# A two-layer decoder trunk with routed experts: weights laid out in load order, one transfer per tile

## The chip, the cores and the metric

The kernel runs on one core of a Trainium2 chip. The metric is device time in microseconds of one execution. The time before is the median of three runs, 851.8 us (851.02 to 852.24).

## What is computed

The reference is a trunk of two layers over 256 tokens of width 1024, in float32. Each layer has a mixer (a combined input projection, a causal convolution branch, a pooling branch, gates, an output projection) and a channel mixer with 32 experts, of which each token uses two. Both are scaled and shifted by vectors that come from `c` through `w_ada`. Cut to what matters:

```python
c_act = jax.nn.silu(c)
for l in range(2):
    sh1, sc1, g1, sh2, sc2, g2 = jnp.split(c_act @ w_ada[l] + b_ada[l], 6, axis=-1)
    proj = modulate(rms_norm(x, mixer_norm_g[l]), sh1, sc1) @ w_in[l]
    u_conv, u_pool, gates = proj[..., :1024], proj[..., 1024:1536], jax.nn.sigmoid(proj[..., 1536:])
    gate_a, gate_b = jnp.split(gates, 2, axis=-1)
    y_a = conformer_conv_branch(u_conv, ...)       # ends in @ w_conv_out
    y_b = pool_branch(u_pool, pool_w[l], pool_scale[l])
    x = x + g1 * ((gate_a * y_a + gate_b * y_b) @ w_out[l])
    t = modulate(rms_norm(x, ffn_norm_g[l]), sh2, sc2)
    # combine: weight of each token for each expert, zero but for two experts of one group
    for e in range(32):
        act = jax.nn.silu(t @ w_expert_gate[l, e]) * (t @ w_expert_up[l, e])
        x = x + g2 * ((act * combine[:, e, None]) @ w_expert_down[l, e])
return rms_norm(x, final_norm_g)
```

The weights are float32 and each is read once; most of the bytes are the experts' (64 experts of 3 MB), then `w_ada`.

## The kernel before

**The stream of weights.** Before any work is written down, `plan` (L84) fills a list, `stream`, with every weight tile of both layers in the order of use. A tile is 128 partitions x 2048 floats, 1 MB. Per layer these are six vectors of `w_ada` at 4 tiles each (`plan_ada`, key `ada`), 14 tiles of `w_in` (`plan_in`, `in`), one of `pool_w` (`pw`), 2 of `w_conv_out` and 4 of `w_out` (`plan_out`, `co`, `wo`), and for each of 16 pairs of experts four gate/up tiles (`gu`, for half h of the contraction and each expert of the pair) and two down tiles (`ed`), by `plan_pair`. Some `ada` tiles of layer 1 stand before layer 0's experts.

**Buffers.** `room` (L92) gives a tile one of 14 ring buffers (`wt` in the profile), or, for expert tiles, one of five work buffers that are idle then (`wx`; the table `SPARE`). `issue` (L102) walks the list in order and writes a transfer on SP's queue for each tile for which there is room; `done` (L122) marks a tile as used and calls `issue` again. So SP's instructions stand in the order of the list, and each waits until the last reader of its buffer has finished. `trickle` puts small loads (rows of biases, the router) between them.

**Form of the transfers.** The host lays out `w_in`, `pool_w` and the small tables (`laid_out`, L1254); the other weights are read from their own arrays. A tile of `w_ada`, `w_conv_out`, `w_out` or `w_expert_down` is one transfer whose rows are two runs of 4 KB per partition. A `gu` tile takes two transfers, one from `w_expert_gate` and one from `w_expert_up`, each of 512 KB with a run of 4 KB per partition; the tile then holds gate and up side by side. The last pair's two down tiles each hold one half of the columns of both experts, in pieces of 2 KB and two transfers.

**Completion semaphores.** Transfers from SP and from ACT signal one of eight semaphores (`DMAHW0` to `DMAHW7`), given in turn in the order in which they are written down, whichever of the two queues issues them. A transfer that gets a semaphore again waits until the one eight places before it has landed.

**The use.** In the mixer each tile is split into two float32r parts on ACT and VectorE or GpSimd (L412, L414) before TensorE uses it in three products. In the experts (`blocks`, L1108, an order written by hand for TensorE, VectorE and ACT) a pair b of experts runs two halves of gate and up products (L1118), SiLU and the product (L1126, L1127), the scatter of the pair before (L1073, L1074), a transpose (L1133), then the down products (L1093). The `gu` tiles of a half are free after that half, the `ed` tiles after the down products.

**`final_norm_g`.** In layer 1, behind pair 5, `final_gain` (L1199) loads `final_norm_g` into the buffer `fz` by a transfer on ACT's queue (L1204). It stands among ACT's instructions of that pair.

**Overflow.** `overflow` holds a branch for tokens beyond an expert's 64 places, with its own weight loads on GpSimd's queue.

Of the kernel before, what the change touches and what calls it, by code (L numbers as in the profile page):

```python
# [29 lines left out]
NE = NG * EPG  # L30
DE = 256
# [17 lines left out]

@with_exitstack  # L50
def trunk(ctx, tc, x, c, w_ada, b_ada, w_in, ada_cols, mix_rows, router, pool_w, w_conv_out, w_out,
          w_expert_gate, w_expert_up, w_expert_down, final_norm_g, out):
# [23 lines left out]
    stream = []  # L76
# [24 lines left out]

    def issue():  # L102
        while state["issued"] < len(stream):
            key, src, (a, b), q = stream[state["issued"]]
            t = room(key, q)
            if t is None:
                return
            v = t[:, :a * b].rearrange("p (a b) -> p a b", b=b)
            if isinstance(src, tuple):
                v = v.rearrange("p (i k) h -> p i k h", i=2)  # L110
                for i, sr in enumerate(src):
                    nc.sync.dma_start(out=v[:, i], in_=sr)
# [11 lines left out]
        issue()  # L124

    def plan_ada(l, m, part=range(4)):
        v = w_ada[l].rearrange("(p k) n -> p k n", k=KC)
        for i in part:
            plan(("ada", l, m, i), v[:, 2 * i:2 * i + 2, m * D:(m + 1) * D], (2, D))

    def plan_in(l, g):
        shape = (KC, 256) if g < 2 else (4, 512)
        for i in range(2):
            yield ("in", l, g, i), w_in[l, 2 * g + i].rearrange("p (a b) -> p a b", b=shape[1]), shape

    def plan_out(l):
        for nm, w, n in (("co", w_conv_out, 2), ("wo", w_out, 4)):
            v = w[l].rearrange("(j p) n -> p j n", p=P)
            for i in range(n):
                plan((nm, l, i), v[:, 2 * i:2 * i + 2, :], (2, D))  # L140

    def plan_pair(l, e):
        ents = []
        for h in range(2):
            for j in range(2):
                ents.append((("gu", l, e + j, h),
                             tuple(w[l, e + j].rearrange("(p k) h -> p k h", k=KC)[:, 4 * h:4 * h + 4, :]
                                   for w in (w_expert_gate, w_expert_up)), (KC, DE)))
        wd = w_expert_down[l, e:e + 2].rearrange("e (j p) n -> p e j n", p=P)
        for j in range(2):  # L150
            if e + 2 < NE:
                ents.append((("ed", l, e + j), wd[:, j], (2, D)))
            else:
                ents.append((("ed", l, e + j), tuple(wd[:, z, :, 512 * j:512 * j + 512] for z in range(2)), (4, 512)))
# [9 lines left out]
    for l in range(DEPTH):  # L164
        for a in pre[l]:
            plan_ada(*a)
        ents = [e for g in groups for e in plan_in(l, g)]
        ents[1], ents[2] = ents[2], ents[1]
        in_seq[l] = [e[0] for e in ents]
        plan_ada(l, 2, range(lead[l]))  # L170
        for n, e in enumerate(ents):
            plan(*e)
            if n == 0:
                plan_ada(l, 2, range(lead[l], 4))
            if n == 12:
                plan(("pw", l), pool_w[l].rearrange("p (g o) -> p g o", o=256), (4, 256))
# [808 lines left out]
    def overflow(l, r, moe):  # L985
# [3 lines left out]
        with (tc.If(flag > 0, label="ov0") if l == 0 else tc.If(flag > 0)):  # L989
# [3 lines left out]
            wsp = r["XTW"][1].rearrange("p a c -> p (a c)")  # L993
# [4 lines left out]
            for tt in range(TT):  # L998
# [9 lines left out]
                                                op0=OP.mult, op1=OP.add)  # L1008
                for e in range(NE):
                    p = pa([P, 2, DE])  # L1010
                    for i, wsrc in enumerate((w_expert_gate, w_expert_up)):
                        wv = wsrc[l, e].rearrange("(p k) h -> p k h", k=KC)
                        for h in range(2):
                            w = wsp.rearrange("p (k h) -> p k h", h=DE)
                            nc.gpsimd.dma_start(out=w, in_=wv[:, 4 * h:4 * h + 4, :])
# [216 lines left out]
    for l in range(DEPTH):  # L1232
# [14 lines left out]


_INS = ['x', 'c', 'w_ada', 'b_ada', 'w_in', 'ada_cols', 'mix_rows', 'router', 'pool_w', 'w_conv_out', 'w_out',
        'w_expert_gate', 'w_expert_up', 'w_expert_down', 'final_norm_g']  # L1250
_OUTS = [((1, SEQ, D), 'float32')]


def laid_out(inputs):  # L1254
# [15 lines left out]
    o = 0  # L1270
# [34 lines left out]
```

## Time and profile before

| | |
|---|---|
| median of 3 runs | 851.8 us |
| profiled execution, its own time | 852.07 us |
| span of the profiled execution | 850.2 us |
| granted TensorE clock, mean | 0.972 |
| PE / VectorE / ACT / GpSimd busy | 778.5 / 505.6 / 277.0 / 198.2 us |
| moved by DMA | 298.39 MB, mean 351 GB/s |

In the order of time: the first vectors of `w_ada` and the norm (to about 35 us), layer 0's mixer (to about 185), routing, layer 0's experts (about 207 to 432), layer 1's mixer (about 444 to 585), routing, layer 1's experts (about 614 to 839), the final norm. [...]

### The profile page before, as it was taken

To read this page: it belongs to the slowest core of one execution; us is meant where nothing else is said; L and a number is where in the kernel's file an instruction comes from. 1 tells how busy PE (TensorE), PEld (TensorE's weight loads), DVE (VectorE), ACT (ScalarE), POOL (GpSimd) and SP (SyncE) were. 2 spreads that over 40 slices of the span, in tenths; PEclk is the share of its full clock that TensorE was granted. 3 is DMA by queue.
4 is the path that set the end of the run, shared out by engine and by line. 5 is a ranking of instruction groups with operands and counts; after the bars stand their busy time and mean duration, and the time that the engine had idled before them with its cause. 6 is when DMAs were issued, how large, how long until landed. Compare 5 with 4: busy or idle time off the path is not lost. (4 is left out here: it accounts for less than half of the span.)

```text
span 850.2 us, 11978 instructions
## 1 busy us (share of the span) xinstructions
PE 778.5 (92%) x4382; PEld 454.4 (53%) x4382; DVE 505.6 (59%) x1023; ACT 277.0 (33%) x494; POOL 198.2 (23%) x133
## 2 busy tenths in 40 slices
PE   4599999997899999999879999999779999999985
PEld 2389986755333433343349998686523333333432
DVE  2369984976344644545376997497734554544545
ACT  2254544434122222222145454543322222222212
POOL 1258972510000000000034898161000000000001
PEclk9699999999999999999989999999889999999998
DMA  9999758969999999999999954797579998999993
GB/s 358 413 421 411 270 174 333 358 238 403 393 409 408 409 410 402 409 409 409 403 417 420 381 182 149 293 385 256 193 264 366 409 405 316 408 410 408 409 408 119
DMA packets 78080, 298.39 MB, mean 351 GB/s; under 512 B 7349, under 2 KB 7861, under 8 KB 74426
## 3 DMA queue, kind: packets, MB, share of 16 engines
q1 hardware_dynamic: 77448, 296.44, 89.6%
q10 hardware_dynamic: 434, 1.06, 0.3%
q8 instruction: 37, 0.61, 0.3%
q14 instruction: 33, 0.27, 0.1%
q0 software_dynamic: 128, 0.02, 0.0%
HBM read 296.44 MB, written 1.05 MB: 350 GB/s over the span
## 5 line engine op out<-in xcount | busy, mean ns | idle before, releaser
L1118 PE MATMUL pb<-wt,XTW 128*64 128x512 f32 x872 | 219.6, 593 | 12.9 <-DMA wt<-in_w_expert_up_dram 8.2
L414 POOL TENSOR_TENSOR wlo<-wt,whi 128x1024 fp32r<-128x1024 f32 x60 | 147.3, 2466 | 88.5 <-ACT whi L412 64.8
L1118 PEld LDWEIGHTS pb<-wt,XTW 128*64 128x64 f32 x872 | 73.6, 137 | 131.3 <-issue 124.5
L1127 DVE SCALAR_TENSOR_TENSOR sl<-sl,rtile,pb 128x256 f32<-128x256 f32 x32 | 15.4, 480 | 164.4 <-ACT sl L1126 164.4
L473 DVE SCALAR_TENSOR_TENSOR pd<-vpad,cols,pd 128x256 f32<-128x256 f32 x232 | 106.9, 488 | 5.7
L412 ACT CAST whi<-wt 128x1024 fp32r<-128x1024 f32 x80 | 82.8, 1049 | 73.8 <-PE pb L352 40.8
L1093 PE MATMUL pd<-wt,aT 128*64 128x512 f32 x360 | 102.7, 618 | 1.8 <-DVE aT L1135 0.5
L1100 ACT CAST yhl<-y 128x512 fp32r<-128x512 f32 x64 | 39.6, 619 | 137.9 <-DVE y L1099 137.9
L351 PE MATMUL pa<-hhl,whi 128*128 128x256 f32 x224 | 66.7, 298 | 5.2 <-ACT hhl L386 5.2
L1126 ACT ACTIVATE sl<-pb 128x256 f32<-128x256 f32 x32 | 12.3, 385 | 172.7 <-PE pb L1118 172.7
L352 PE MATMUL pa<-hhl,whi 128*128 128x256 f32 x224 | 65.6, 293 | 0.3
L353 PE MATMUL pa<-hhl,wlo 128*128 128x256 f32 x224 | 64.5, 288 | 0.6 <-POOL wlo L414 0.6
L351 PE MATMUL pb<-hhl,whi 128*128 128x256 f32 x224 | 63.6, 284 | 0.0
L297 PE MATMUL pd<-wt,cb 128*32 128x512 f32 x384 | 51.4, 623 | 13.1 <-DMA wt<-in_w_ada_dram 13.0
L352 PE MATMUL pb<-hhl,whi 128*128 128x256 f32 x224 | 62.7, 280 | 0.0
L353 PE MATMUL pb<-hhl,wlo 128*128 128x256 f32 x224 | 62.6, 279 | 0.0
L1093 PEld LDWEIGHTS pd<-wt,aT 128*64 128x64 f32 x360 | 29.1, 141 | 59.4 <-issue 39.2
L1104 DVE TENSOR_TENSOR yhl<-y,yhl 128x512 fp32r<-128x512 f32 x64 | 44.3, 693 | 22.0 <-ACT yhl L1100 22.0
L392 POOL MEMSET vpad<- 128x120 f32 x2 | 0.4, 200 | 242.5 <-DVE sl L1127 242.5
L1118 PE MATMUL pb<-wx,XTW 128*64 128x512 f32 x152 | 55.1, 593 | 0.0
L1093 PE MATMUL pd<-wx,aT 128*64 128x512 f32 x152 | 52.7, 610 | 0.8 <-DVE aT L1135 0.5
L1099 DVE TENSOR_TENSOR y<-pd,gb 128x512 f32<-128x512 f32 x64 | 44.0, 688 | 15.4 <-PE pd L1093 15.4
(257 smaller groups left out, 1345.5 us busy)
## 6 DMA issues: line engine op xcount, KB each, us to landing
wt<-in_w_expert_gate_dram SPq DMA_DIRECT2D x109, 512.0 KB, 11.5
wt<-in_w_expert_up_dram SPq DMA_DIRECT2D x109, 512.0 KB, 12.8
wt<-in_w_ada_dram SPq DMA_DIRECT2D x48, 1024.0 KB, 13.7
wt<-in_w_expert_down_dram SPq DMA_DIRECT2D x41, 1024.0 KB, 11.7
wt<-in_w_in_dram SPq DMA_DIRECT2D x28, 1024.0 KB, 20.1
wx<-in_w_expert_down_dram SPq DMA_DIRECT2D x19, 1024.0 KB, 12.0
wx<-in_w_expert_gate_dram SPq DMA_DIRECT2D x19, 512.0 KB, 11.1
wx<-in_w_expert_up_dram SPq DMA_DIRECT2D x19, 512.0 KB, 10.2
```

The lines of the kernel that those rows point to most:

```text
L297: nc.tensor.matmul(ps[j:j + 32, :], cb[:, 2 * i + a, :], halves(w[:, a, :], h), start=i == 0, stop=i == 3)
L351: nc.tensor.matmul(o, ah, bh, start=start, stop=False, skip_group_check=True)
L352: nc.tensor.matmul(o, ah, bl, start=False, stop=False, skip_group_check=True)
L353: nc.tensor.matmul(o, al, bh, start=False, stop=stop, skip_group_check=True)
L412: nc.scalar.copy(hi, wv)
L414: eng.tensor_tensor(lo, wv, hi.bitcast(F32), op=OP.subtract)
L473: nc.vector.scalar_tensor_tensor(acc[:, j, :] if t == CONV_K - 1 else a, src, w, a, op0=OP.mult, op1=OP.add)
L1093: nc.tensor.matmul(o[64 * j:64 * j + 64, :], aTs[b][:, h, 64 * j:64 * j + 64], wv[j][:, h, :], start=h == 0, stop=h == 1)
L1099: nc.vector.tensor_tensor(y, downs.pop(n), s["g2"][:, n * 512:(n + 1) * 512], op=OP.mult)
L1100: nc.scalar.copy(ys[b][0][:, n * 512:(n + 1) * 512], y)
L1104: nc.vector.tensor_tensor(yl, downs.pop(("y", n)), yh.bitcast(F32), op=OP.subtract)
L1118: nc.tensor.matmul(p[64 * j:64 * j + 64], XT[:, k, 64 * j:64 * j + 64], w[j][:, :, kk, :], start=k == 0, stop=k == KC - 1)
```

## The change

Four more groups of weights are laid out by the host in the order in which they are loaded: each tile is one block of 128 x 2048 floats, so 8 KB per partition in one run. `w_expert_gate` and `w_expert_up` become one array, `w_gate_up`; `w_expert_down` becomes `w_down`, with the last pair's column halves already exchanged. `issue` writes one transfer per tile, for `gu` tiles too. The loads in the overflow branch follow the new arrays. The stream, its order, the buffers and the views of a tile that the products read stay as they are. The core of the diff:

```diff
     def issue():
         while state["issued"] < len(stream):
-            key, src, (a, b), q = stream[state["issued"]]
+            key, src, shape, q = stream[state["issued"]]
             t = room(key, q)
             if t is None:
                 return
-            v = t[:, :a * b].rearrange("p (a b) -> p a b", b=b)
-            if isinstance(src, tuple):
-                v = v.rearrange("p (i k) h -> p i k h", i=2)
-                for i, sr in enumerate(src):
-                    nc.sync.dma_start(out=v[:, i], in_=sr)
-            else:
-                nc.sync.dma_start(out=v, in_=src)
+            v = t[:, :src.shape[-1]]
+            nc.sync.dma_start(out=v, in_=src)
+            v = v.rearrange(*(("p (a b) -> p a b",) if len(shape) == 2 else ("p (i a b) -> p i a b",)),
+                            **dict(zip("ab" if len(shape) == 2 else "iab", shape)))
             tiles[key] = v
...
     def plan_ada(l, m, part=range(4)):
-        v = w_ada[l].rearrange("(p k) n -> p k n", k=KC)
         for i in part:
-            plan(("ada", l, m, i), v[:, 2 * i:2 * i + 2, m * D:(m + 1) * D], (2, D))
+            plan(("ada", l, m, i), w_ada[l, m, i], (2, D))
...
     def plan_pair(l, e):
-        ents = []
-        for h in range(2):
-            for j in range(2):
-                ents.append((("gu", l, e + j, h),
-                             tuple(w[l, e + j].rearrange("(p k) h -> p k h", k=KC)[:, 4 * h:4 * h + 4, :]
-                                   for w in (w_expert_gate, w_expert_up)), (KC, DE)))
...
+        ents = [(("gu", l, e + j, h), w_gate_up[l, e + j, h], (2, 4, DE))
+                for h in range(2) for j in range(2)]
+        ents += [(("ed", l, e + j), w_down[l, e + j], (2, D) if e + 2 < NE else (2, 2, 512)) for j in range(2)]
...
+    v = a["w_ada"].reshape(DEPTH, P, 4, 2, 6, D).transpose(0, 4, 2, 1, 3, 5)
+    r["w_ada"] = v.reshape(DEPTH, 6, 4, P, 2048)
+    for k in ("w_conv_out", "w_out"):
+        r[k] = a[k].reshape(DEPTH, -1, 2, P, D).transpose(0, 1, 3, 2, 4).reshape(DEPTH, -1, P, 2048)
+    gu = np.stack([a[k].reshape(DEPTH, NE, P, 2, 4 * DE) for k in ("w_expert_gate", "w_expert_up")], 4)
+    gu = np.ascontiguousarray(gu.transpose(0, 1, 3, 2, 4, 5)).reshape(DEPTH, NE, 2, P, 2048)
+    r["w_gate_up"] = gu
```

Transfers written on SP's and ACT's queues fall from 432 to 300, and with that the semaphores fall on other transfers. On SP, in layer 1 behind pair 5, before the change; the names are the buffers' (numbers keep them apart), in brackets are the semaphores waited for:

```order
L112 DMA wt_11622<-in_w_expert_up_dram 128x1024 [waits DMAHW0_49]
L112 DMA wt_11625<-in_w_expert_gate_dram 128x1024 [waits DMAHW2_49,PE_49]
L112 DMA wt_11625<-in_w_expert_up_dram 128x1024 [waits DMAHW3_49]
L112 DMA wt_11636<-in_w_expert_gate_dram 128x1024 [waits DMAHW4_49,PE_49]
L112 DMA wt_11636<-in_w_expert_up_dram 128x1024 [waits DMAHW5_49]
L112 DMA wt_11639<-in_w_expert_gate_dram 128x1024 [waits DMAHW6_49,PE_49]
L112 DMA wt_11639<-in_w_expert_up_dram 128x1024 [waits DMAHW7_49]
L114 DMA wt_11712<-in_w_expert_down_dram 128x2x1024 [waits DMAHW0_49,PE_49]
L114 DMA wx_11714<-in_w_expert_down_dram 128x2x1024 [waits DMAHW1_49,PE_49]
```

`DMAHW1` is missing between the first two rows: the transfer of `fz` on ACT's queue has it. The last row is the next to use it, so it waits for `fz`; four tiles stand between. The same place on SP after the change:

```order
L109 DMA wt_11544<-in_w_gate_up_dram 128x2048 [waits DMAHW1_49,PE_49]
L109 DMA wt_11546<-in_w_gate_up_dram 128x2048 [waits DMAHW3_49,PE_49]
L109 DMA wt_11556<-in_w_gate_up_dram 128x2048 [waits DMAHW4_49,PE_49]
L109 DMA wt_11558<-in_w_gate_up_dram 128x2048 [waits DMAHW5_49,PE_49]
L109 DMA wt_11630<-in_w_down_dram 128x2048 [waits DMAHW6_49,PE_49]
L109 DMA wx_11632<-in_w_down_dram 128x2048 [waits DMAHW7_49,PE_49]
L109 DMA wx_11643<-in_w_gate_up_dram 128x2048 [waits DMAHW0_49,PE_49]
L109 DMA wt_11645<-in_w_gate_up_dram 128x2048 [waits DMAHW1_49,PE_49]
L109 DMA wt_11655<-in_w_gate_up_dram 128x2048 [waits DMAHW2_49,PE_49]
```

Now `fz` has `DMAHW2`, and the next to use it stands three tiles further on: `wx_11632` is the tile that `wx_11714` was. On ACT, the place of `fz` itself, before the change:

```order
L1056 COPY XTW_8331<-XTp_8003 128x4x64
L1100 CAST yhl_11793<-y_11804 128x512 [waits DVE_49,Activation_49]
L1100 CAST yhl_11793<-y_11811 128x512 [waits DVE_49]
L1204 DMA fz_11819<-in_final_norm_g_dram 1x1024 [waits DMAHW5_49,DMAHW6_49,DMAHW1_49,Pool_49]
L1126 ACTIVATE sl_11851<-pb_11822 128x256 [waits PE_49]
```

And after it, where it stands behind the same two casts of pair 5 (L1100 is now L1090):

```order
L1046 COPY XTW_8260<-XTp_7937 128x4x64
L1090 CAST yhl_11707<-y_11718 128x512 [waits DVE_49,Activation_49]
L1090 CAST yhl_11707<-y_11725 128x512 [waits DVE_49]
L1194 DMA fz_11733<-in_final_norm_g_dram 1x1024 [waits DMAHW3_49,DMAHW2_49,Pool_49]
L1116 ACTIVATE sl_11761<-pb_11736 128x256 [waits PE_49]
```

ACT's rows have not moved against each other; only the lines' numbers and the semaphores differ.

## Rows read from the trace of the kernel before

**Rows 1.** The page: busy time, DMA packets, the queue of GpSimd's transfers.

```profile
PE 778.5 (92%) x4382; PEld 454.4 (53%) x4382; DVE 505.6 (59%) x1023; ACT 277.0 (33%) x494; POOL 198.2 (23%) x133
DMA packets 78080, 298.39 MB, mean 351 GB/s; under 512 B 7349, under 2 KB 7861, under 8 KB 74426
q0 software_dynamic: 128, 0.02, 0.0%
```

**Rows 2.** Windows: the expert stages, then the arrival of `w_in`; columns first.

```profile
core 0: us, PE busy (x) PEld busy (x) DVE busy (x) ACT busy (x) POOL busy (x), PEclk, DMA share, GB/s
220.00:421.00 201.00, 193.58 (x861) 75.86 (x860) 99.55 (x184) 46.25 (x106) 0.00 (x0) 0.99 1.03 408
716.00:826.00 110.00, 106.97 (x471) 42.41 (x469) 53.41 (x96) 25.48 (x58) 0.00 (x0) 1.00 1.03 409
44.00:56.00 12.00, 12.00 (x104) 9.20 (x103) 6.23 (x6) 8.22 (x9) 8.27 (x4) 1.00 1.02 424
440.00:456.00 16.00, 13.74 (x88) 11.17 (x89) 10.72 (x15) 9.54 (x13) 8.52 (x5) 0.79 1.02 422
```

**Rows 3.** Chain that ended last: down projections of layer 1 (start, us, what).

```profile
671.36 3.65 PE pd L1093 x16
...
684.22 3.65 PE pd L1093 x16
...
709.91 1.94 PE pd L1093 x8
```

**Rows 4.** Timeline of PE, both expert stages: start, us, instruction, [idle before, releaser].

```profile
381.78 3.65 PE L1093 MATMUL pd<-wx,aT 128*64 128x512 f32 x16
...
421.80 3.62 PE L1118 MATMUL pb<-wt,XTW 128*64 128x512 f32 x14 [1.47 <-DMA wt<-in_w_expert_up_dram]
...
427.74 3.65 PE L1093 MATMUL pd<-wt,aT 128*64 128x512 f32 x16
...
813.56 3.62 PE L1118 MATMUL pb<-wt,XTW 128*64 128x512 f32 x14 [1.47 <-DMA wt<-in_w_expert_up_dram]
...
828.93 3.62 PE L1118 MATMUL pb<-wt,XTW 128*64 128x512 f32 x14 [1.47 <-DMA wt<-in_w_expert_up_dram]
...
834.89 3.65 PE L1093 MATMUL pd<-wt,aT 128*64 128x512 f32 x16
```

**Rows 5.** Timelines of SP and ACT around `fz`; last, SP's wait (total, times, longest).

```profile
693.64 0.38 SPq L114 DMA_DIRECT2D wt<-in_w_expert_down_dram  x1
703.47 0.38 SPq L114 DMA_DIRECT2D wx<-in_w_expert_down_dram  x1
...
701.94 0.49 ACTq L1204 DMA_DIRECT2D fz<-in_final_norm_g_dram  x1
...
SPq L114 <- DMA fz<-in_final_norm_g_dram: 9.4, 1, 9.4
```

**Rows 6.** Windows: a slow restart, then the slices around the wait for `fz`.

```profile
638.00:650.00 12.00, 11.95 (x56) 4.63 (x54) 6.22 (x12) 2.52 (x6) 0.00 (x0) 1.00 0.95 342
700.00:702.00 2.00, 2.00 (x12) 0.72 (x10) 1.74 (x3) 0.64 (x2) 0.00 (x0) 1.00 0.68 272
702.00:704.00 2.00, 2.00 (x12) 0.60 (x10) 0.69 (x1) 0.42 (x1) 0.00 (x0) 1.00 0.08 27
704.00:706.00 2.00, 2.00 (x12) 0.70 (x10) 0.00 (x0) 0.00 (x0) 0.00 (x0) 1.00 0.62 162
708.00:710.00 2.00, 1.95 (x12) 1.25 (x12) 1.65 (x4) 1.29 (x5) 0.00 (x0) 1.00 0.88 317
710.00:718.00 8.00, 8.00 (x38) 2.69 (x40) 5.03 (x9) 1.42 (x3) 0.00 (x0) 1.00 0.95 355
```

**Rows 7.** Timelines of PE and ACT at the start.

```profile
27.54 1.69 PE L297 MATMUL pd<-wt,cb 128*32 128x512 f32 x8 [1.48 <-DMA wt<-in_w_ada_dram]
...
35.44 0.58 PE L351 MATMUL pa<-hhl,whi 128*128 128x256 f32 x1 [4.39 <-ACT hhl L386]
...
11.26 0.63 ACT L340 ACTIVATE xn<-xs 128x512 f32<-128x512 f32 x1 [1.39 <-DMA xs<-in_x_dram]
```

More of the change, by code (lines that the diff above doesn't have):

```diff
@@ L51, in trunk @@
 def trunk(ctx, tc, x, c, w_ada, b_ada, w_in, ada_cols, mix_rows, router, pool_w, w_conv_out, w_out,
-          w_expert_gate, w_expert_up, w_expert_down, final_norm_g, out):
+          w_gate_up, w_down, final_norm_g, out):
     nc = tc.nc
@@ L126, in plan_ada @@
     def plan_ada(l, m, part=range(4)):
-        v = w_ada[l].rearrange("(p k) n -> p k n", k=KC)
         for i in part:
-            plan(("ada", l, m, i), v[:, 2 * i:2 * i + 2, m * D:(m + 1) * D], (2, D))
+            plan(("ada", l, m, i), w_ada[l, m, i], (2, D))
     def plan_in(l, g):
-        shape = (KC, 256) if g < 2 else (4, 512)
         for i in range(2):
-            yield ("in", l, g, i), w_in[l, 2 * g + i].rearrange("p (a b) -> p a b", b=shape[1]), shape
+            yield ("in", l, g, i), w_in[l, 2 * g + i], (KC, 256) if g < 2 else (4, 512)
     def plan_out(l):
         for nm, w, n in (("co", w_conv_out, 2), ("wo", w_out, 4)):
-            v = w[l].rearrange("(j p) n -> p j n", p=P)
             for i in range(n):
-                plan((nm, l, i), v[:, 2 * i:2 * i + 2, :], (2, D))
+                plan((nm, l, i), w[l, i], (2, D))
     def plan_pair(l, e):
-        ents = []
-        for h in range(2):
-            for j in range(2):
-                ents.append((("gu", l, e + j, h),
-                             tuple(w[l, e + j].rearrange("(p k) h -> p k h", k=KC)[:, 4 * h:4 * h + 4, :]
-                                   for w in (w_expert_gate, w_expert_up)), (KC, DE)))
[L149 to L154, printed above, removed]
+        ents = [(("gu", l, e + j, h), w_gate_up[l, e + j, h], (2, 4, DE))
+                for h in range(2) for j in range(2)]
+        ents += [(("ed", l, e + j), w_down[l, e + j], (2, D) if e + 2 < NE else (2, 2, 512)) for j in range(2)]
         for i, (key, src, shape) in enumerate(ents):
@@ L175, in trunk @@
             if n == 12:
-                plan(("pw", l), pool_w[l].rearrange("p (g o) -> p g o", o=256), (4, 256))
+                plan(("pw", l), pool_w[l], (4, 256))
         for a in late[l]:
@@ L1010, in overflow @@
                     p = pa([P, 2, DE])
-                    for i, wsrc in enumerate((w_expert_gate, w_expert_up)):
-                        wv = wsrc[l, e].rearrange("(p k) h -> p k h", k=KC)
+                    for i in range(2):
                         for h in range(2):
                             w = wsp.rearrange("p (k h) -> p k h", h=DE)
-                            nc.gpsimd.dma_start(out=w, in_=wv[:, 4 * h:4 * h + 4, :])
+                            nc.gpsimd.dma_start(out=wsp, in_=w_gate_up[l, e, h, :, 4 * DE * i:4 * DE * (i + 1)])
                             for kk in range(4):
@@ L1029, in overflow @@
                     for h in range(2):
-                        nc.gpsimd.dma_start(out=wsp, in_=w_expert_down[l, e].rearrange("(j p) n -> p j n", p=P)[:, h])
+                        if e < NE - 2:
+                            nc.gpsimd.dma_start(out=wsp, in_=w_down[l, e, :, D * h:D * (h + 1)])
+                        else:
+                            z = (2 * (e - NE + 2) + h) * 512
+                            for n in range(2):
+                                nc.gpsimd.dma_start(out=wsp[:, n * 512:(n + 1) * 512],
+                                                    in_=w_down[l, NE - 2 + n, :, z:z + 512])
                         for n in range(2):
@@ L1249 @@
 _INS = ['x', 'c', 'w_ada', 'b_ada', 'w_in', 'ada_cols', 'mix_rows', 'router', 'pool_w', 'w_conv_out', 'w_out',
-        'w_expert_gate', 'w_expert_up', 'w_expert_down', 'final_norm_g']
+        'w_gate_up', 'w_down', 'final_norm_g']
 _OUTS = [((1, SEQ, D), 'float32')]
@@ L1282, in laid_out @@
     r["pool_w"] = a["pool_w"].transpose(0, 2, 1, 3).reshape(DEPTH, P, 4 * 256)
+    v = a["w_ada"].reshape(DEPTH, P, 4, 2, 6, D).transpose(0, 4, 2, 1, 3, 5)
[5 more added lines that the diff above has]
+    r["w_gate_up"] = gu
+    v = a["w_expert_down"].reshape(DEPTH, NE, 2, P, D).transpose(0, 1, 3, 2, 4)
+    wd = np.ascontiguousarray(v).reshape(DEPTH, NE, P, 2048)
+    for n in range(2):
+        wd[:, NE - 2 + n] = v[:, NE - 2:, :, :, 512 * n:512 * n + 512].transpose(0, 2, 1, 3, 4).reshape(DEPTH, P, 2048)
+    r["w_down"] = wd
     return r
```

## Prediction

> **What bounds the kernel now.** The page comes first: TensorE (PE) is busy 778.5 of 850.2 us, and 298.39 MB are moved [rows 1]. Neither fills the span alone, so the question is which of the two ends last in each stage. The windows by stage answer the DMA half: from 220 to 421 us and from 716 to 826 us, the two expert stages, the DMA share is 1.03, so all 16 engines always have work, at 408 and 409 GB/s; from 44 to 56 us and from 440 to 456 us, where the tiles of `w_in` arrive, the share is 1.02 and the rate 424 and 422 GB/s [rows 2]. `w_in` is the one weight whose tiles lie 8 KB per partition already; all others are read in rows of 4 KB. The page's packet line agrees: 78,080 packets less 74,426 under 8 KB leaves 3,654, and 28 tiles of `w_in` times 128 partitions are 3,584 [rows 1].
>
> The chain of waits answers the other half. In layer 1's experts the down projections of consecutive pairs stand at 671.36, 684.22 and 709.91 us (one pair between the last two left out): 12.85 us a pair, all PE [rows 3]. A pair needs 6 tiles of 1.049 MB, which at 409 GB/s take 6 x 2.564 = 15.4 us. So PE is faster than its supply: it lives for some pairs on what the ring holds, and waits after that. The PE timeline shows it: the second half of L1118 waits for the up weights at 421.80 in layer 0 and at 813.56 and 828.93 in layer 1, 15.37 us apart, the DMA's pace [rows 4].
>
> How much waiting is there to win? Layer 0: from the down at 381.78 three PE-paced pairs would end at 381.78 + 3 x 12.85 = 420.3; it starts at 427.74, so 7.4 us [rows 4]. Layer 1: from 709.91 nine pairs would give 825.6; it starts at 834.89, so 9.3 us [rows 3, 4]. The mixers between these stages have hardly a wait for DMA; their tiles are consumed more slowly than they come.
>
> **The change, part by part.**
> *Packets of 8 KB.* A tile takes 2.564 us at 409 GB/s and 2.485 us at 422: 0.079 us saved per tile, wherever the stream runs without a gap into a wait. The bounds are 0 (the rate stays 409) and 0.09 (424); I take 422, the longer of the two windows, since the new tiles have exactly the form of `w_in`'s.
> - Start: 8 tiles of `w_ada` stand before the scales of the first norm; PE waits 1.48 us for the last of them at 27.54, and the first mixer product follows at 35.44 [rows 7]. 8 x 0.079 = **0.6 us**. One thing is against it: x comes on ACT's queue in 4 KB rows and shares the engines with SP's packets. If turns go by packet, x gets a third in place of a half, and its second part (read at 11.26, [rows 7]) comes up to 2.5 us later. The wait for `w_ada` covers that; without the cover it costs 2.5 us.
> - Layer 0: the stream has no gap from 220 to the wait at 421.80. 201 / 2.564 = 78 tiles, 78 x 0.079 = **6.2 us**, under the 7.4 us that PE allows.
> - Layer 1: from the restart at 638 to the wait at 828.93 are 191 us. Less 5.3 us for a hole (next point) and 2.0 us for the slow restart 638 to 650 (342 in place of 409 GB/s, [rows 6]) that is 184 us, 71 tiles, 71 x 0.079 = 5.6 us.
>
> *One transfer per tile, and with it other lanes.* A gate/up tile was two issues of 512 KB and becomes one. SP was never short of time (0.4 us an issue [rows 5], 2.5 us a tile), so the fewer issues save nothing by themselves. But transfers of SP and ACT share eight completion semaphores in turn, and a transfer waits for the eighth before it. The load of `final_norm_g` (`fz`) is one of them: ACT issues it in its own order, behind pair 5, at 701.94, and SP's next user of that semaphore waits for it: 9.4 us, from 693.64 to 703.47 [rows 5]. Before, four tiles stand between the two, after the change seven (the rows of the order show it). What the hole costs: 272, 27 and 162 GB/s in the slices from 700 to 706 are (137 + 382 + 247) x 2 / 409 = 3.75 us of stream; the slow restart at 317 and 355 GB/s another 0.45 + 1.06 us [rows 6]. Together 5.3 us. With three tiles more already queued (7.5 us of work) the engines would run dry at about 701 + 7.5 = 708.5, after the 705.2 at which a transfer issued at 703.47 flows (162 GB/s in the slice 704 to 706 are 0.8 us of flow, [rows 6]). Their buffers are free in time: they held tiles of pairs 4 and 5, and pair 4's down ends by 688. So the hole closes: 5.3 us, bounds 0 and 5.3.
> - Layer 1 together: 5.6 + 5.3 = 10.9 us of stream, but PE has only 9.3 us of waiting. What is late next is PE itself, at 12.85 us a pair. I take **9.0 us**: the stream then arrives 1.6 us before PE needs it, and a small stall may show.
>
> *Deeper queue.* Eight in flight are 8.4 MB in place of about 5. A tile is issued earlier only if its buffer is free, and the tiles ahead of it are needed earlier; so nothing is delayed. PE's, VectorE's and ACT's instructions keep their order and their addresses in the tile. The last pair's pieces of 2 KB become 8 KB, but the two down tiles land after the wait that counts and before their use: 0. The overflow branch, whose loads are rewritten, does not run: the software queue moves 0.02 MB in all [rows 1].
>
> **Sum:** 0.6 + 6.2 + 9.0 = 15.8 us. The profiled execution's span of 850.2 us becomes 834.4, its 852.07 us becomes 836.3; against the median of 851.8 us that is **836.0 us**.
>
> **The rivals.**
> 1. *The hole only moves.* `fz` is issued at PE's pace, and SP is held until then in any case. If the queue holds less than I count (a buffer later, or `fz` itself lands late behind full queues), the engines run dry again. For it: only some 3 us of margin. Against: seven tiles in place of four. Layer 1 then keeps 5.6 us: 0.6 + 6.2 + 5.6 = 12.4, 839.4 us; with a still longer hole up to 841.
> 2. *The rate lies between.* In the expert stages something other than the packet may take part. With half the difference (0.04 us a tile): 0.3 + 3.1 + min(9.3, 5.3 + 2.8) = 11.5, 840.3 us. Against it: share and tile form in the rows of `w_in`.
> 3. *The change does not do what it says to the rate:* memory sets it, or the 8 KB are cut into 4 KB. Then only the hole closes: 846.5 us. Against it stands the packet count, and two windows at 422 and 424. [...]
> 4. *Slower.* After each gap the same 4 KB stream runs at 342 or 355 GB/s for ten microseconds at a share of 0.95 [rows 6], so the memory can give less to a fed queue. If the new layout kept the engines in that state through the expert stages, even half of that drop (382 GB/s, 2.745 us a tile) costs 0.181 x 149 = 27 us less the 5.3: 873 us. It decides from about 403 GB/s, where 149 x 0.036 us eat the closed hole. Against: `w_in` streams long at 422.
>
> [...]
>
> **How the numbers follow.** Chances: forecast (834 to 838) 0.60; rival 1 0.14; rival 2 0.11; rival 3 0.08; rival 4 0.04; within 0.2% (1.7 us, about what a measurement of this kernel can tell from no change) 0.03. Faster by over 0.2%: 0.60 + 0.14 + 0.11 + 0.08 = 0.93. The range goes from the sum of all bounds, 0.9 + 7.4 + 9.3 = 17.6 us or 834, to 843, which takes in rivals 1 and 2 and leaves 3 and 4 out.
>
> **What would show it.** Right: 420 GB/s or more in the expert stages, and 8 KB packets; PE's waits for gate/up in layer 0 shrunk to at most one or two pairs and gone or nearly so in layer 1; no slice under 350 GB/s near 690 us; down projections 12.85 us apart to the end; layer 1's experts starting about 7 us earlier. Wrong: a rate of 409 (rival 3), a dry queue behind `fz` (rival 1), or a first mixer product later than 35.4 us (x).

## The result, and the profile after

The changed kernel takes 837.56 us (median of 4 runs, 836.95 to 839.18) where the kernel before takes 851.41 on the same chip (4 runs, 848.66 to 852.24): a ratio of 0.9846, 95% interval 0.9819 to 0.9872. That is 13.9 us faster, beyond the 0.2% that a measurement can tell from no change. 836.0 was forecast, with a range of 834 to 843. The profiled execution has a span of 835.8 us where that of before had 850.2.

First the page of the changed kernel: the busy times, the packets, and the chain of work that ended last, by engine.

```profile
PE 776.1 (93%) x4382; PEld 452.7 (54%) x4382; DVE 504.1 (60%) x1023; ACT 276.7 (33%) x494; POOL 199.2 (24%) x133
...
DMA packets 42687, 298.37 MB, mean 357 GB/s; under 512 B 5237, under 2 KB 5749, under 8 KB 6778
...
PE 24%; DVE 2%; ACT 0%; issue 0%; DVEq 0%; POOL 0%; ACTq 0%
```

The same bytes go in 42,687 packets instead of 78,080 [rows 1], and only 6,778 of them are under 8 KB. The chain of work that ended last, which in both kernels reaches back over about a quarter of the span, holds no DMA now; before, DMA was half of it:

```profile
DMA 13%; PE 11%; DVE 2%; ACT 0%; issue 0%; DVEq 0%; POOL 0%; ACTq 0%; SPq 0%
```

The windows of the changed kernel show the rate (the last column) in the experts of layer 0, where `w_in` arrives for layer 1, in the experts of layer 1, and just behind the first experts of layer 1. Then come three slices around the load of `fz`. PEclk is the granted TensorE clock as a share of the full clock, DMA share the mean busy share of the 16 DMA engines.

```profile
core 0: us, PE busy (x) PEld busy (x) DVE busy (x) ACT busy (x) POOL busy (x), PEclk, DMA share, GB/s
240.00:400.00 160.00, 159.38 (x724) 62.11 (x722) 84.34 (x153) 38.74 (x90) 0.00 (x0) 1.00 1.01 421
434.00:450.00 16.00, 12.77 (x80) 10.20 (x80) 11.45 (x15) 8.94 (x12) 8.44 (x4) 0.79 1.02 421
718.00:805.00 87.00, 86.66 (x390) 33.44 (x386) 42.79 (x78) 20.61 (x46) 0.00 (x0) 1.00 1.01 421
632.00:644.00 12.00, 11.96 (x58) 4.68 (x56) 6.30 (x12) 3.14 (x7) 0.00 (x0) 1.00 1.01 426
...
696.00:698.00 2.00, 2.00 (x12) 0.69 (x10) 0.00 (x0) 0.00 (x0) 0.00 (x0) 1.00 0.89 367
698.00:700.00 2.00, 2.00 (x12) 0.46 (x8) 0.00 (x0) 0.00 (x0) 0.00 (x0) 1.00 0.58 115
700.00:702.00 2.00, 2.00 (x11) 1.56 (x10) 1.08 (x2) 1.00 (x3) 0.00 (x0) 1.00 0.83 340
```

The experts now get 421 GB/s, exactly the rate of `w_in`'s tiles, where they had 408 and 409 [rows 2]. The slow restart of layer 1 (342 GB/s, [rows 6]) is gone as well. The stop behind `fz` isn't: the slices from 696 to 702 us lack (54 + 306 + 81) x 2 / 421 = 2.1 us of stream.

What TensorE sees of it stands in its timeline: three pairs of downs near the end of layer 0's experts, the last of them, with one pair's gate/up products between, and the last of layer 1 (start, us, instruction).

```profile
384.16 3.65 PE L1083 MATMUL pd<-wx,aT 128*64 128x512 f32 x16
...
409.86 3.65 PE L1083 MATMUL pd<-wt,aT 128*64 128x512 f32 x16
413.35 7.04 PE L1108 MATMUL pb<-wt,XTW 128*64 128x512 f32 x32
422.71 3.65 PE L1083 MATMUL pd<-wt,aT 128*64 128x512 f32 x16
...
820.30 3.65 PE L1083 MATMUL pd<-wt,aT 128*64 128x512 f32 x16
```

No row carries a wait for a DMA, and the 32 gate/up products of a pair are one unbroken group of 7.04 us; before they were split by a wait of 1.47 us [rows 4]. From 384.16 to 422.71 are exactly three times 12.85 us. Layer 0's last down is 5.0 us earlier than the 427.74 of before [rows 4], layer 1's 14.6 us earlier than 834.89. TensorE, not the stream, sets the end of both stages now.

| place | before, us | after, us | gain so far |
|---|---|---|---|
| first mixer product, layer 0 | 35.44 | 31.85 | 3.6 |
| TensorE resumes after the first half of the gather, layer 0 | 199.77 | 198.51 | 1.3 |
| first gate/up product, layer 0 | 207.42 | 209.09 | -1.7 |
| last pair of downs, layer 0 | 427.74 | 422.71 | 5.0 |
| first gate/up product, layer 1 | 614.18 | 608.36 | 5.8 |
| last pair of downs, layer 1 | 834.89 | 820.30 | 14.6 |

The table compares one profile with one profile. The lengths of the experts' stages repeat: layer 0's experts, from the first product to the last downs, take 219.2 to 221.3 us in the four profiles with 4 KB packets, and 213.2 to 214.8 us in the seven with 8 KB packets at the full rate. The starts of the stages scatter more, as the runs below show.

One line of the table was not foreseen: more than the start had won was lost before the experts of layer 0 began. The windows of the changed kernel and TensorE's timeline show where (columns as above).

```profile
112.00:116.00 4.00, 4.00 (x20) 3.76 (x19) 3.89 (x10) 0.59 (x1) 3.45 (x2) 0.57 0.02 4
...
198.00:200.00 2.00, 1.49 (x2) 0.84 (x3) 0.37 (x1) 0.00 (x0) 0.00 (x0) 0.50 1.00 410
200.00:202.00 2.00, 2.00 (x3) 0.57 (x2) 0.00 (x0) 0.59 (x1) 0.00 (x0) 0.50 1.02 426
202.00:204.00 2.00, 2.00 (x11) 1.94 (x10) 0.34 (x2) 0.59 (x1) 0.00 (x0) 0.50 0.95 397
...
198.51 3.75 PE L305 MATMUL pd<-part,Q 128*128 128x512 f32 x4 [2.98 <-DVE part L293]
202.06 1.06 PE L311 MATMUL pt<-idc,part 128*128 128x128 f32 x4
202.77 2.98 PE L829 MATMUL pd<-G,xhl 128*128 128x256 f32 x16
```

The first window and the same three groups in the kernel before:

```profile
112.00:116.00 4.00, 2.02 (x10) 1.28 (x10) 3.82 (x10) 2.59 (x5) 4.00 (x3) 1.00 0.59 239
...
199.77 1.96 PE L320 MATMUL pd<-part,Q 128*128 128x512 f32 x4 [3.00 <-DVE part L308]
201.56 0.63 PE L326 MATMUL pt<-idc,part 128*128 128x128 f32 x4
201.95 2.14 PE L844 MATMUL pd<-G,xhl 128*128 128x256 f32 x16
```

The wait ahead of the groups is the same (2.98 and 3.00 us), but afterwards the changed kernel's TensorE runs at a granted clock of 0.50, and the three groups end 7.2 us after the first began instead of 4.3. That is the 2.9 us between a lead of 1.3 and a lag of 1.7. The stretch from 112 to 116 us, at 0.57 where the kernel before had 1.00, is short of (1 - 0.57) x 4 = 1.7 us at the full clock; by this estimate it took a part of the 2.3 us that were lost earlier.

### The profile page after: what moved, and what is told of

Read it like the earlier page. It is cut to its first block, busy times and chain, and to the rows that moved or that the text cites. A ratio compares the mean times of both kernels' runs of the same rounds, so it can differ in the third digit from the quotient of the medians.

```text
span 835.8 us, 11843 instructions
## 1 busy us (share of the span) xinstructions
PE 776.1 (93%) x4382; PEld 452.7 (54%) x4382; DVE 504.1 (60%) x1023; ACT 276.7 (33%) x494; POOL 199.2 (24%) x133
## 2 busy tenths in 40 slices
DMA packets 42687, 298.37 MB, mean 357 GB/s; under 512 B 5237, under 2 KB 5749, under 8 KB 6778
## 5 line engine op out<-in xcount | busy, mean ns | idle before, releaser
L1108 PE MATMUL pb<-wt,XTW 128*64 128x512 f32 x872 | 213.2, 593 | 5.2 <-ACT XTW L1046 2.9
L1108 PEld LDWEIGHTS pb<-wt,XTW 128*64 128x64 f32 x872 | 69.6, 137 | 121.2 <-issue 115.0
L1090 ACT CAST yhl<-y 128x512 fp32r<-128x512 f32 x64 | 39.6, 619 | 137.0 <-DVE y L1089 137.0
L336 PE MATMUL pa<-hhl,whi 128*128 128x256 f32 x224 | 67.4, 301 | 3.3 <-ACT hhl L371 3.3
L337 PE MATMUL pa<-hhl,whi 128*128 128x256 f32 x224 | 66.6, 298 | 1.1 <-DVE hhl L373 1.0
L282 PE MATMUL pd<-wt,cb 128*32 128x512 f32 x384 | 54.0, 655 | 9.0 <-DVE cb L220 6.7
## 6 DMA issues: line engine op xcount, KB each, us to landing
wx<-in_w_down_dram SPq DMA_DIRECT2D x19, 1024.0 KB, 12.4
```

What stands on the lines that cost most here:

```text
L282: nc.tensor.matmul(ps[j:j + 32, :], cb[:, 2 * i + a, :], halves(w[:, a, :], h), start=i == 0, stop=i == 3)
L336: nc.tensor.matmul(o, ah, bh, start=start, stop=False, skip_group_check=True)
L337: nc.tensor.matmul(o, ah, bl, start=False, stop=False, skip_group_check=True)
L1090: nc.scalar.copy(ys[b][0][:, n * 512:(n + 1) * 512], y)
L1108: nc.tensor.matmul(p[64 * j:64 * j + 64], XT[:, k, 64 * j:64 * j + 64], w[j][:, :, kk, :], start=k == 0, stop=k == KC - 1)
```

## The experiments

Two things changed at once: the packets went from 4 to 8 KB, and a gate/up tile went from two transfers to one. The prediction put 6.2 us of layer 0 and 5.6 us of layer 1's stream on the first, and the 5.3 us of the stop behind `fz` on the second. The runs take these apart. Ratios are to the kernel before on the same chip, which had medians of 851.4 to 852.0 us.

### The stop behind fz alone, and one transfer alone

Kernel before, `fz` on another queue:

```diff
-            nc.scalar.dma_start(out=fin_g["row"][0:1, :], in_=final_norm_g.rearrange("(a n) -> a n", a=1))
+            nc.gpsimd.dma_start(out=fin_g["row"][0:1, :], in_=final_norm_g.rearrange("(a n) -> a n", a=1))
```

> The kernel before, with one word changed: the load of final_norm_g into fz goes out on POOL's queue instead of ACT's, so that no transfer of the stream on SP has to wait for it. Packets stay at 4 KB. Theory A (the prediction's: the stop of the stream at 700 us comes from SP waiting for fz, and is worth 5.3 us of its own): the slice with no bytes near 704 us is gone, the experts of layer 1 end about 5.3 us earlier, layer 0 is unchanged with its pair waits at 421.8 and 427.7 us; time 846.1, ratio 0.994. Rival B (the stop is made good later, or another transfer takes fz's place, so that only the packet size counts): within 0.2% of the kernel before, 851.4.

Measured: 847.38 us, ratio 0.9951 (0.9934 to 0.9967). The windows of this kernel:

```profile
240.00:400.00 160.00, 158.38 (x713) 61.29 (x714) 83.53 (x151) 37.30 (x85) 0.00 (x0) 1.00 1.03 409
...
698.00:702.00 4.00, 4.00 (x22) 1.31 (x20) 3.03 (x7) 1.24 (x2) 0.00 (x0) 1.00 1.03 413
702.00:706.00 4.00, 4.00 (x22) 1.42 (x20) 0.44 (x1) 0.00 (x0) 0.00 (x0) 1.00 1.02 403
```

The slices that held 27 GB/s [rows 6] are full, at the old rate. From its first gate/up product (613.73) to its last downs (828.95) layer 1 takes 215.2 us; before it took 220.7. The stop was worth 5.5 us; 5.3 had been counted. Rival B falls.

Kernel before, gate and up stored one behind the other and fetched by one transfer:

```diff
-                             tuple(w[l, e + j].rearrange("(p k) h -> p k h", k=KC)[:, 4 * h:4 * h + 4, :]
-                                   for w in (w_expert_gate, w_expert_up)), (KC, DE)))
+                             w_gate_up[l, e + j].rearrange("i p c -> p i c")[:, :, 4 * DE * h:4 * DE * (h + 1)],
+                             (KC, DE)))
```

> The kernel before, with gate and up of an expert stored one behind the other by the host and each gate/up tile fetched by one transfer of 1 MB; the runs in memory stay at 4 KB. This is one transfer per tile without the longer packets. Theory A (the packet size sets the rate): 408 to 410 GB/s in the experts of both layers, as before; layer 0 ends where it did (last pair of downs at 427.7 us). With whole tiles on each completion semaphore there are more bytes queued ahead of the transfer that waits for fz, so the stop at 704 us shrinks by 2 to 4 us: time 847.5 to 849.5, ratio 0.995 to 0.998. Rival B (fewer, larger transfers make the rate): 419 to 422 GB/s and a time near the changed kernel's 837.6.

Measured: 844.3 us, ratio 0.9910 (0.9893 to 0.9926), more than theory A allowed. The windows of this kernel, and a wait of TensorE:

```profile
240.00:400.00 160.00, 159.37 (x720) 61.57 (x720) 84.99 (x153) 37.99 (x88) 0.00 (x0) 1.00 1.03 409
...
637.00:649.00 12.00, 11.96 (x58) 4.65 (x55) 6.37 (x12) 3.14 (x7) 0.00 (x0) 1.00 1.02 404
...
702.00:706.00 4.00, 4.00 (x20) 1.63 (x17) 0.38 (x1) 0.38 (x1) 0.00 (x0) 1.00 0.99 368
...
820.85 3.62 PE L1121 MATMUL pb<-wt,XTW 128*64 128x512 f32 x14 [0.54 <-DMA wt<-in_w_gate_up_dram]
```

The rate is 409 GB/s, as theory A said: fewer transfers don't make it, and rival B falls. But two things went further than expected. Of the stop 0.4 us is left in the slice from 702 to 706 us (368 in place of 409 GB/s). And the slow restart, 342 GB/s for twelve microseconds in the kernel before [rows 6], is gone at the same 4 KB packets (404 GB/s). Layer 1's experts take 213.5 us, 7.3 us less than before, with one wait of 0.54 us for a transfer left in the last pair (820.85 us); layer 0's last downs come at 426.83, 0.9 us earlier.

### Two transfers with 8 KB packets

Changed kernel, each gate/up tile by two transfers, lower and upper half of the partitions:

```diff
-            nc.sync.dma_start(out=v, in_=src)
+            if key[0] == "gu":
+                for i in range(2):
+                    nc.sync.dma_start(out=v[64 * i:64 * i + 64], in_=src[64 * i:64 * i + 64])
+            else:
+                nc.sync.dma_start(out=v, in_=src)
```

> The changed kernel, with each gate/up tile fetched by two transfers of 512 KB again, split by partitions (0 to 63, 64 to 127), so that the packets stay at 8 KB. This is the longer packet without one transfer per tile. Theory A: 419 to 422 GB/s, layer 0 as in the changed kernel (last pair of downs at about 422.7 us, no wait for a transfer), and the stop of the stream behind fz returns with its 3 to 5 us in layer 1, of which TensorE sees up to 3 us since the stream is ahead there: 837.6 to 840.5, ratio 0.984 to 0.987. Rival B: 408 to 410 GB/s and 846 to 851.

Measured: 1182.39 us, ratio 1.387 (1.380 to 1.395). Neither theory had this. The window in the middle of layer 0's experts, and the page's packets:

```profile
300.00:340.00 40.00, 27.75 (x91) 9.52 (x91) 12.73 (x23) 5.36 (x13) 0.00 (x0) 0.90 1.02 233
...
DMA packets 44736, 298.39 MB, mean 253 GB/s; under 512 B 7285, under 2 KB 7797, under 8 KB 8826
```

The packets are 8 KB and all 16 engines are busy (share 1.02), yet they move 233 GB/s instead of 421. So the run says nothing on the number of transfers: the split itself brought a cost. The next run keeps the count and the packet and changes only which partitions belong together.

```diff
-                    nc.sync.dma_start(out=v[64 * i:64 * i + 64], in_=src[64 * i:64 * i + 64])
+                    nc.sync.dma_start(out=v.rearrange("(a i) c -> i a c", i=2)[i], in_=src.rearrange("(a i) c -> i a c", i=2)[i])
```

> The changed kernel with each gate/up tile again fetched by two transfers of 512 KB with 8 KB packets, split by even and odd partitions instead of lower and upper half. In the run with halves the stream fell to 233 GB/s between 300 and 340 us, and the time rose to 1182 us. Theory D (a transfer whose rows all lie in 64 neighbouring partitions is slow, the number of transfers is not): 418 to 422 GB/s in the experts, 837.6 to 840.5 us. Rival E (any transfer of 64 rows is slow): 230 to 260 GB/s and 1150 to 1200 us.

Measured: 854.49 us, a single run. The windows of this kernel, and SP's wait (total, times, longest):

```profile
240.00:400.00 160.00, 159.37 (x724) 62.06 (x722) 83.45 (x151) 38.50 (x89) 0.00 (x0) 1.00 1.01 421
...
680.00:698.00 18.00, 17.95 (x84) 6.68 (x82) 9.90 (x18) 4.29 (x9) 0.00 (x0) 1.00 0.01 3
...
SPq L111 <- DMA fz<-in_final_norm_g_dram: 26.4, 1, 26.4
```

On the rate theory D holds: 421 GB/s with two transfers of 64 rows, so it was the block of 64 neighbouring partitions that cost 188 GB/s. With odd and even partitions the same count, size and packet kept the full rate. Why the block is slower no run shows.

On the time theory D missed by 14 us, and the rows say why: the stop behind `fz` is back, and much longer than it ever was. SP waits 26.4 us, and for 18 us next to nothing moves (3 GB/s). That this is all of it was put to a run with both edits, this split and `fz` on POOL's queue:

> The kernel with two transfers per gate/up tile by odd and even partitions (8 KB packets), which took 854.5 us, with the load of final_norm_g on POOL's queue besides. Theory A (those 17 us are the stop of the stream behind fz alone, where SP waits 26.4 us and the queue is empty from 680 to 698 us): 421 GB/s without a stop, 837.6 us within 0.3%, as the changed kernel. Rival H (two transfers per tile cost time of their own, for instance through SP's issuing): 845 us or more.

Measured: 837.24 us, ratio 0.9822 (0.9798 to 0.9847), and the window in place of the stop:

```profile
690.00:700.00 10.00, 9.98 (x48) 3.36 (x48) 5.14 (x9) 1.34 (x3) 0.00 (x0) 1.00 1.01 417
```

Theory A holds. Two transfers per tile cost nothing measurable by themselves: the ratio is 0.9822 with two and 0.9817 with one on the same chip (the repetition below). In the kernel with the stop SP's last issue was at about 670 us and the engines ran dry 9 us later; in the changed kernel they had 13 us of work at that point. So the reading is that transfers of half the size bring SP to the semaphore that it shares with `fz` earlier and with less queued ahead.

### What is left of the stop in the changed kernel

The changed kernel with `fz` on POOL's queue (the first diff of this section, on it):

> The changed kernel with the load of final_norm_g on POOL's queue. Theory A (after the change TensorE and not the stream sets the end of layer 1's experts, so that the rest of the stop behind fz costs nothing): the slice with 98 GB/s near 699 us is gone, the downs of layer 1 stay 12.85 us apart, time 837.6 within 0.2%. Rival C (the rest of the stop still costs): 835 to 836.

Measured: 837.64 us, ratio 0.9837 (0.9818 to 0.9855), where the changed kernel has 837.56. The slice that held 115 GB/s:

```profile
698.00:700.00 2.00, 2.00 (x12) 0.57 (x8) 0.00 (x0) 0.00 (x0) 0.00 (x0) 1.00 1.04 426
```

The stop is gone and the time is the same, as theory A said: the 2.1 us that the stream still lost cost nothing. Rival C falls.

### Smaller packets

Changed kernel, the host lays each gate/up tile out as four planes, so that one transfer has runs of 2 KB:

```diff
-            v = t[:, :src.shape[-1]]
-            nc.sync.dma_start(out=v, in_=src)
+            if key[0] == "gu":
+                v = t[:, :]
+                nc.sync.dma_start(out=v.rearrange("p (s c) -> p s c", s=4), in_=src.rearrange("s p c -> p s c"))
+            else:
+                v = t[:, :src.shape[-1]]
+                nc.sync.dma_start(out=v, in_=src)
```

> The changed kernel with each gate/up tile laid out by the host as four planes, so that its one transfer has runs of 2 KB. Tiles of down keep 8 KB. Theory A (each packet costs a fixed time beside its bytes: 4 KB to 8 KB takes 8 packets fewer per engine and tile and saved 0.079 us, 9.9 ns a packet): a gate/up tile takes 2.564 + 16 x 0.0099 = 2.722 us, a pair of experts 4 x 2.722 + 2 x 2.485 = 15.86 instead of 14.91 us, 397 GB/s in the experts; 13 pairs in layer 0 and 11.8 in layer 1 make 12.4 and 11.3 us, less up to 2 us each in which TensorE and not the stream sets the end now: 857 to 861 us. Rival G (the gain of 8 KB is a step of its own and below it the rate is flat at 409): 413 GB/s and 841 to 846 us.

Measured: 854.09 us, ratio 1.0027 (1.0005 to 1.0048). Its rate in the experts of layer 0, and two of TensorE's waits there:

```profile
240.00:400.00 160.00, 157.61 (x705) 61.28 (x703) 81.42 (x148) 37.77 (x88) 0.00 (x0) 1.00 1.04 397
...
409.83 3.62 PE L1113 MATMUL pb<-wt,XTW 128*64 128x512 f32 x14 [1.53 <-DMA wt<-in_w_gate_up_dram]
425.62 3.62 PE L1113 MATMUL pb<-wt,XTW 128*64 128x512 f32 x14 [1.66 <-DMA wt<-in_w_gate_up_dram]
```

The rate is the 397 GB/s of theory A, and pairs that wait come 15.79 us apart (15.86 expected); rival G's 413 falls. The time is 3 us below theory A's 857. Layer 0 lost 10.8 us (224.4 in place of 213.6 from first product to last downs; 12.4 less up to 2 expected). Layer 1 lost 6.6. If the stream lost the expected 11.3 there, it was 11.3 - 6.6 = 4.7 us ahead of TensorE in the changed kernel, not 2; this is an estimate.

Three runs now give the pace of a pair that waits for its tiles: 15.79 us with gate/up in runs of 2 KB, 15.37 with 4 KB (828.93 - 813.56, [rows 4]), and 14.88 us with 8 KB (822.27 to 837.15 in the odd/even kernel, behind its stop). At 2.485 us for each down tile, a gate/up tile takes (15.79 - 4.97) / 4 = 2.70 us in the first, and a tile 15.37 / 6 = 2.56 and 14.88 / 6 = 2.48 us in the others. A tile has 512, 256 and 128 runs; taken as packets and spread evenly over the 16 engines, these are 32, 16 and 8 for an engine. By this estimate a packet costs 0.14 / 16 = 9 and 0.08 / 8 = 10 ns beside its bytes: nearly the same price over both steps.

### One half of the change at a time

The changed kernel with `w_ada`, `w_conv_out` and `w_out` read as before, in rows of 4 KB (plan_ada here; plan_out and the host's part alike):

```diff
+        v = w_ada[l].rearrange("(p k) n -> p k n", k=KC)
         for i in part:
-            plan(("ada", l, m, i), w_ada[l, m, i], (2, D))
+            plan(("ada", l, m, i), v[:, 2 * i:2 * i + 2, m * D:(m + 1) * D], (2, D))
```

> The changed kernel with w_ada, w_conv_out and w_out left in their old order in memory (runs of 4 KB, one transfer per tile as before); only the experts' tiles have the new layout. Theory A (in the mixers the stream is ahead and waits for buffers, only the first 27 us depend on it): 837.6 to 838.4 us. Rival F (faster tiles of the mixers also bring the experts' first tiles earlier): 840 us or more.

Measured: 836.87 us, ratio 0.9821 (0.9791 to 0.9852). The opposite, the kernel before with those three alone in the new layout:

> The kernel before with the new layout for w_ada, w_conv_out and w_out alone; the experts' tiles stay as they were. Theory A: 850.2 to 851.9 us, within 0.2% of the kernel before, with the stop at 704 us and the pair waits at 421.8 and 427.7 us as before. Rival F: 846 to 849 us.

Measured: 850.99 us, ratio 0.9986 (0.9970 to 1.0001). The first is 0.7 us below theory A's range, away from rival F's 840; the second lies in it. What can be measured of the gain comes from the experts' tiles, and rival F falls.

### The clock ahead of the experts

The changed kernel once more, and with two lines exchanged, so that TensorE gathers through the wait of 2.98 us:

```diff
         gather(0)
-        flush()
         gather(1)
+        flush()
```

> The changed kernel itself once more, for the comparison with the run that exchanges the two lines, and for a second look at the clock. Theory A: 837.6 us within 0.2%; the stretches at half the clock between 183 and 205 us come again, with other lengths, and the experts of layer 0 begin between 207 and 210 us. Rival J (the stretches were an accident of one execution): clock 1.00 from 150 to 210 us, the experts begin at about 206 us and the time is 835 us.

> The changed kernel with two lines exchanged where the experts begin: the second half of the gather of the tokens goes ahead of the flush of the adaLN rows, which makes TensorE wait 2.98 us for VectorE at 195.5 us (and the same in layer 1), after which its granted clock was 0.50 from 198 to 204 us in the changed kernel. Theory A (the experts of layer 0 began 1.7 us later than in the kernel before, though the mixers ended 1.25 us earlier, because of that stretch at half the clock, and TensorE now bounds the experts): the first gate/up product of layer 0 comes 2 to 5 us earlier than 209.09 us, the experts of both layers keep 12.85 us a pair, and the time is 831 to 836 us. Rival I (what is won ahead of the experts is lost to waits for the stream behind them): 837.6 us within 0.2%.

Measured for the repetition: 836.05 us, ratio 0.9817 (0.9796 to 0.9838). Its experts begin at 209.02, and its clock from 198 to 204 us is 0.50 again:

```profile
198.00:204.00 6.00, 5.56 (x14) 3.42 (x15) 0.64 (x3) 1.17 (x2) 0.00 (x0) 0.50 0.98 403
```

So the stretch repeats, and as an accident of one execution, rival J, it is out. It needn't come in every execution: of the five runs of the repetition the two with a mean clock of 0.968 and 0.972 took 837.4 and 837.7 us, the three with 0.979 took 834.9 to 836.1, near rival J's 835. The profile is that of the run of 837.4 us. With the lines exchanged: 831.43 us, ratio 0.9758 (0.9739 to 0.9777). The windows and TensorE's timeline of this kernel:

```profile
198.00:200.00 2.00, 1.27 (x11) 1.07 (x10) 1.60 (x4) 1.18 (x4) 0.00 (x0) 1.00 1.06 434
200.00:202.00 2.00, 1.28 (x3) 0.68 (x4) 0.67 (x1) 0.45 (x2) 0.00 (x0) 1.00 0.96 401
202.00:204.00 2.00, 1.17 (x6) 0.63 (x4) 0.61 (x4) 1.36 (x3) 0.00 (x0) 1.00 1.04 434
...
200.72 1.98 PE L305 MATMUL pd<-part,Q 128*128 128x512 f32 x4 [1.45 <-DVE part L293]
204.15 2.36 PE L1108 MATMUL pb<-wt,XTW 128*64 128x512 f32 x8 [0.98 <-ACT XTW L1046]
```

The clock stays at 1.00, the group that took 3.75 us takes 1.98, and the experts begin 4.9 us earlier, at 204.15. The stages behind keep it in the main: the last downs of layer 0 come at 418.90 (422.67 in the repetition), those of layer 1 at 814.04 (820.04). Theory A holds, and this is the fastest of the kernels: 20 us under the kernel before.

What makes the clock fall there isn't settled. The kernel before has the same wait, 3.00 us, and keeps 1.00, and so do the other kernels with the experts' tiles in 4 KB packets (1.00 in every window from 195 to 210 us). In the changed kernel with `fz` on POOL's queue the fall is shorter (the first group takes 3.42 us, the experts begin at 207.72), and also with the new layout for the experts alone (2.70 us, 208.52). The two odd/even kernels differ only in the load of `fz`, far behind this place, and TensorE resumes at 199.44 and 199.50 us in them after the same wait of 2.99 us. Their windows, the second with `fz` on POOL's queue:

```profile
200.00:204.00 4.00, 4.00 (x9) 1.90 (x8) 0.00 (x0) 1.17 (x2) 0.00 (x0) 0.50 1.01 416
...
200.00:204.00 4.00, 4.00 (x27) 3.28 (x26) 1.34 (x4) 1.27 (x3) 0.00 (x0) 1.00 1.03 422
```

The experts begin at 210.04 in the first and at 207.16 in the second. So the same instructions ran through this place with the fall in one execution and without it in another, and the packet size alone doesn't decide it. What is shown is that the fall costs 2.9 us, here and in the result. Of the 4.9 us that the exchange gave, about 2.0 are then, by this estimate, the work that now fills the wait. That filling the wait keeps the clock up rests on a single profile and isn't shown, since the clock also stayed up without it.

## Why the prediction was right, point by point

- *What bounds the kernel.* Right. The stream's rate, 408 and 409 GB/s [rows 2], bounded the ends of both expert stages. With 421 GB/s all waits for DMA there went, and the pairs run at the 12.85 us that the chain of waits had shown [rows 3].
- *Packets of 8 KB, 0.079 us a tile.* Right: 421 GB/s (2.491 us a tile) against the 422 taken from `w_in`'s windows, and one transfer per tile with 4 KB packets stays at 409. The price per packet, an estimate of 9 to 10 ns from the paces of a pair, held at 2 KB too. Rivals 2, 3 and 4, which put the rate lower, fall. From 409 to 421 GB/s are 2.9%.
- *Layer 0, 6.2 us.* 6.7 us (220.3 to 213.6 from first product to last downs). No pair waited any more, where one or two had been allowed for.
- *The stop behind `fz` closes.* This step was wrong in its mechanism and right in its effect. The engines were to run dry 3.3 us after a released transfer flows again, on the strength of three more tiles queued, seven in all. SP's last issue was at 684.37 us and the engines ran dry at about 697.7: 13.3 us of work, five tiles. And `fz`, issued at 694.5, released SP only at 698.45, 4.0 us later. In the kernel before and in the odd/even kernel, where the engines were dry by then, this took 1.5 [rows 5] and 1.4 us, so the reading is that the small transfer stood behind full queues here. SP's wait grew from 9.4 to 13.6 us:

```profile
SPq L109 <- DMA fz<-in_final_norm_g_dram: 13.6, 1, 13.6
...
684.37 14.88 SPq L109 DMA_DIRECT2D wt<-in_w_gate_up_dram  x3
...
698.45 0.80 SPq L109 DMA_DIRECT2D wt<-in_w_gate_up_dram  x2
```

  So rival 1's mechanism was there in small: 2.1 us of stream are still lost, and the sign "no slice under 350 GB/s near 690 us" was not met (115). It cost nothing, because the cap held; with the margin of 1.6 us that was counted, 2.1 us would have shown.
- *Layer 1, 10.9 us of stream capped to 9.0 by TensorE.* 8.8 us (220.7 to 211.9). The cap is what made the sum robust: the stop alone gives 5.5 us, one transfer per tile alone 7.3, and the packets only the rest. The margin behind the cap was mis-sized, luckily on the safe side: 1.6 us were counted, the kernel with runs of 2 KB puts it at 4.7, by the estimate given there. The slow restart, which the prediction had kept as a loss of 2.0 us, went away: with single transfers of 4 KB packets it is gone (404 GB/s), and with two transfers of 8 KB packets too (412 and 421 GB/s from 631 to 643 us in the odd/even kernel with `fz` on POOL's queue). It was seen in two kernels whose tiles come in two transfers of 4 KB packets: 342 GB/s in the kernel before [rows 6], 382 and then 337 from 638 to 650 us with `fz` on POOL's queue. Whether the memory gives less there, as rival 4 had it, no run shows.
- *Start, 0.6 us.* The size was off, and the sign at the experts. TensorE's timeline at the start:

```profile
16.18 0.66 PE L353 MATMUL pa<-idc,xn 128*128 128x128 f32 x2 [4.35 <-DVE xn L345]
...
26.84 1.07 PE L282 MATMUL pd<-wt,cb 128*32 128x512 f32 x8 [0.72 <-DMA wt<-in_w_ada_dram]
...
31.85 0.58 PE L336 MATMUL pa<-hhl,whi 128*128 128x256 f32 x1 [2.49 <-ACT hhl L371]
```

  The last wait for `w_ada` ended 0.7 us earlier (26.84 for 27.54, [rows 7]), as worked out, and x did come later (ACT reads its second part at 13.41 us for 11.26, [rows 7]), covered: TensorE waits 4.35 us at 16.18. The first mixer product came 3.6 us earlier, more than the transfers account for. Most of that is scatter: the kernel before with `fz` on POOL's queue, which is the same up to there, has it at 32.74, 2.7 us ahead of the kernel before. And what arrived at the experts was -1.7 us, through the 2.9 us at half the clock; in the profiles with 8 KB packets at the full rate and these lines in their old order the experts begin between 207.16 and 210.04, with 4 KB between 206.68 and 207.66. This is the term that failed: +0.6 was forecast, -1.7 measured in this pair of profiles, and the scatter is larger than the term. The mixers of layer 1, counted at 0, gave 0.8 us; the sign "layer 1's experts starting about 7 us earlier" came out at 5.8.

The sum over the table is -1.7 + 6.7 + 0.8 + 8.8 = 14.6 us of the 15.8 forecast; the span fell by 14.4. In the sum of all bounds the start stands with 0.9 us, where eight tiles at 0.09 us make 0.7; the lower end of 834 stays the same.

## What to carry to other kernels

A stream that is read in 4 KB rows while one tensor of the same kernel already comes in 8 KB rows has its own price list in the trace: compare the windows, and take the packet's price from them. Cap what a faster stream can give by the pace of the engine it feeds; here the cap, not the stream, was the figure that held when two effects overlapped (9.0 us counted, 8.8 measured). Look for the small load on another queue that shares its completion semaphores with the stream: here moving it took the kernel with tiles cut in two by odd and even partitions from 854.49 to 837.24 us and the kernel before from 851.97 to 847.38, and did nothing once the stream was ahead (837.56 and 837.64).

## What the runs showed of the hardware that was not expected

- Transfers of 64 neighbouring partitions, in the same 8 KB packets, moved 233 GB/s at a DMA share of 1.02; odd and even partitions moved 421.
- A 4 KB load on ACT's queue held SP for 9.4, 13.6 or 26.4 us, depending on how the stream's transfers were cut; at 26.4 us the stream was next to empty for 18 us (3 GB/s from 680 to 698 us).
- After a wait of 2.99 us TensorE went on at a clock of 1.00 from 200 to 204 us in one execution and at 0.50 in another with the same instructions up to there, and began the experts 2.9 us later (210.04 for 207.16).
- A stream of two 512 KB transfers per tile in 4 KB packets came back at 342 GB/s for 12 us after a gap (638 to 650 us); with 1 MB transfers (404) or 8 KB packets (412 to 426) it did not.
